# Moving the start addresses of the activation tiles in a transformer-block kernel

## The chip, the core and the metric

The kernel runs as one program on one core of a Trainium2 chip. The core has TensorE (PE; its weight loads are listed apart as PEld), VectorE (DVE), ScalarE (ACT), GpSimd (POOL) and SyncE (SP, which issues the transfers). The metric is device microseconds of one execution, lower is better. The profile comes from one further execution of the same program, taken by the hardware profiler.

## What is computed

One transformer block on 256 tokens of width 1024, all in float32: an adaptive norm whose scales, shifts and gates come from `silu(c) @ w_ada + b_ada`, a wide input projection, causal attention with eight heads of 64, a gated spatial unit, two projections and an output product with a gated residual, a second adaptive norm, a feed-forward part of width 4096 with squared ReLU, and a final norm.

```python
h = rmsnorm(x, g_mix) * (1 + scale1) + shift1
q, k, v, u, vs, ga, gb = split(h @ w_in)
y_attn = moba_attention(q, k, v) @ w_proj_attn
y_sgu  = spatial_gating(gelu(u), gelu(vs), ...) @ w_proj_sgu
x = x + gate1 * ((sigmoid(ga) * y_attn + sigmoid(gb) * y_sgu) @ w_out)
h = rmsnorm(x, g_ffn) * (1 + scale2) + shift2
x = x + gate2 * (square(relu(h @ w_ff1)) @ w_ff2)
return rmsnorm(x, g_final)
```

## The kernel before

**Products in three passes.** Each large product is made in `float32r`. A streamed weight tile `raw` of 128 x 2048 values (8,192 bytes in each partition) is rounded by ACT to `whi`, and DVE writes the rest, `raw - whi`, to `wlo`. An activation is held as such a pair too (`hh`/`hl`, `oh`/`ol`, `yh`/`yl`, `mh`/`ml`, `zh`/`zl`, `fh`/`fl`). `mm3` (L69) then issues three matmuls for one 128 x 128 block of weights: `whi` with the high part, `whi` with the low part, `wlo` with the high part. The weights are the stationary operand, and 256 columns of activations (one per token) move past them; in the feed-forward's first product it is 258 columns. So 48 matmuls belong to one streamed tile.

**The stages, in the order of the program.** First a loop over eight slices of `w_in` (L276), in which weights arrive, norm coefficients are formed, and the slice's products for q, k, v and the gate's input accumulate in eight PSUM banks; the products for v and vs have the weights as the moving operand, 512 columns each. Then ten products `n` = 0 to 9 from `hh`/`hl` (L480 on), with attention scores, exponentials, transposes and the attention's second product in between. Then four steps (n = 10 to 13) from `oh`/`ol` and `yh`/`yl`, four (n = 14 to 17) from `mh`/`ml`, and the feed-forward: 16 first products from `zh`/`zl` (`ff1`, L596) alternating with 16 second products from `fh`/`fl` (`ff2`, L628). At the end the final norm and the output.

**Order and buffers.** In the first loop and at the very end the order is the one written; in between a scheduler places the instructions, `prepare(n + 2)` (L257) making the weights of two steps later. There are five `raw` buffers, four of `whi`, three of `wlo` and eight PSUM banks (`bank`, L59). SP issues every transfer.

**Where tiles stand.** Pools are laid out one behind the other in the order in which they are opened (L51 to L56), and within a pool the tags stand in the order in which each is first asked for. A tile takes its bytes per partition, rounded up to 32. In `act` that order is `xt`/`gb_sb`/`zl` (tag b4, 8,256 bytes because of the 258 columns), `x_sb`, `hh`/`mh` (b1), `hl`/`ml` (b2), `xn`/`ga_sb`/`zh` (b3, 8,256 bytes as well), then the tiles q1, q2, v, vs, u1, o1 and o2. In `wk` it is `pt`/`fl`, `hf`, `t512b`, four `acc` of 4 bytes, `t512a`, `pr`/`fh`, and other small tiles, after which `raw`, `whi` and `wlo` begin. The profile shows no addresses; the numbers below are those of the built program.

In this text a line is 64 bytes, and the line of an address is its place among the 16 lines of 1,024 bytes. The rows of an activation tile are 1,024 bytes apart, so each row starts at the tile's own line; those of `zh` and `zl` are 1,032 bytes apart and wander by 8 bytes from one to the next. A block of 128 weights takes 512 bytes, so weights start at line 7 or line 15.

Of the kernel before, what the change touches and what calls it, by code (L numbers as in the profile page):

```python
# [9 lines left out]
F32 = mybir.dt.float32  # L10
# [6 lines left out]
P = 128  # L17
S = 256
D = 1024
KT = D // P  # L20
# [27 lines left out]
def block_kernel(ctx, tc, x, xT, cols, wsguT, bsgu, w_a1, w_1, w_a, w_m, w_f, out):  # L48
# [2 lines left out]
    const = ctx.enter_context(tc.tile_pool(name="const", bufs=1))  # L51
    act = ctx.enter_context(tc.tile_pool(name="act", bufs=1))
    wk = ctx.enter_context(tc.tile_pool(name="wk", bufs=2))
    raws = ctx.enter_context(tc.tile_pool(name="raws", bufs=5))
    his = ctx.enter_context(tc.tile_pool(name="his", bufs=4))
    los = ctx.enter_context(tc.tile_pool(name="los", bufs=3))  # L56
# [5 lines left out]
    def load(src, pieces=1):  # L62
        t = raws.tile([P, 2048], F32, name="raw", tag="raw")
        n = 2048 // pieces
        for i in range(pieces):
            nc.sync.dma_start(out=t[:, n * i:n * i + n], in_=src[:, n * i:n * i + n])
        return t
# [12 lines left out]
    for t in range(2):  # L80
        nc.sync.dma_start(out=xt[:, t, 0:D], in_=x[t])
        DVE.memset(xt[:, t, D:D + 1], (EPS * D) ** 0.5)
    x_sb = act.tile([P, KT, S], F32, name="x_sb")
    ada = {0: load(w_a1[0], 2)}
    wraw = {0: load(w_1[0], 4)}
# [33 lines left out]
                      stop=last, skip_group_check=t == 1)  # L119

    def rstd(o, n):
        ms = wk.tile([P, 2], F32, name="ms", tag="ms")
        ACT.activation(out=ms, in_=o[:, 0:2], func=AF.Identity, scale=1.0 / n, bias=eps)
        rs = wk.tile([P, 2], F32, name="rs", tag="rs")
        nc.gpsimd.tensor_tensor(out=rs, in0=ms, in1=nhalf, op=ALU.pow)
        return rs

# [50 lines left out]

    def dot(raw, i):
        junk = wk.tile([P, D], BF16, name="junk", tag="t512b")  # L180
        acc = wk.tile([P, 1], F32, name="acc", tag="acc", bufs=4)
        DVE.scalar_tensor_tensor(
            out=junk, in0=raw[:, D * i:D * i + D], scalar=0.5, in1=csb, op0=ALU.mult, op1=ALU.mult, accum_out=acc)
        return acc
# [76 lines left out]
    def ada_dots(m, half):  # L261
        i = (0, 4, 1, 5, 2, 6, 3, 7, 8, 9, 10, 11, 12, 13, 14, 15)[m]
        if half == 0:
            raw_of["d", m] = fetch("a", m)
        raw = raw_of["d", m]
        column(dot(raw, half), (SCALE2, GATE1, SHIFT2, GATE2)[i // 4], 2 * (i % 4) + half)
# [1 line left out]

    hh = act.tile([P, KT, S], F32R, name="hh", tag="b1")
    hl = act.tile([P, KT, S], F32R, name="hl", tag="b2")  # L270
    xn = act.tile([P, KT, S], F32, name="xn", tag="b3")
    wsg = const.tile([P, 8, P], F32, name="wsg", tag="c4")
    bsg = const.tile([P, NP, P], F32, name="bsg")
    qk_ps = [bank() for _ in range(4)]
# [1 line left out]
    for kt in range(KT):  # L276
# [22 lines left out]


        da = dot(raw, 0)
        if f:
            column(da, SCALE1, kt)
        db = dot(raw, 1)
        w_hi(0)
        if not f:
# [100 lines left out]

    def attn_exp(banks):
        pr = wk.tile([P, 2, 3 * P], F32, name="pr", tag="pr", bufs=3)
        sm = wk.tile([P, 2, 2], F32, name="sm", tag="sm", bufs=2)  # L410
        for i in range(2):
            b = banks[i]
            mx = wk.tile([P, 2], F32, name="mx", tag="mx", bufs=4)
            DVE.tensor_reduce(out=mx[:, 0:1], in_=b[:, 0:S], axis=AX.X, op=ALU.max, negate=True)
            DVE.tensor_reduce(out=mx[:, 1:2], in_=b[:, S:S + P], axis=AX.X, op=ALU.max, negate=True)
            ACT.activation(out=pr[:, i, 0:S], in_=b[:, 0:S], func=AF.Exp, bias=mx[:, 0:1],
                           accum_out=sm[:, i, 0:1])
            ACT.activation(out=pr[:, i, S:S + P], in_=b[:, S:S + P], func=AF.Exp, bias=mx[:, 1:2],
                           accum_out=sm[:, i, 1:2])
        return pr, sm  # L420

    def attn_norm(pr, sm):
        rc = wk.tile([P, 2, 2], F32, name="rc", tag="rc", bufs=2)
        DVE.reciprocal(out=rc, in_=sm)
        for i in range(2):
            ACT.activation(out=pr[:, i, 0:S], in_=pr[:, i, 0:S], func=AF.Copy, scale=rc[:, i, 0:1])
            ACT.activation(out=pr[:, i, S:S + P], in_=pr[:, i, S:S + P], func=AF.Copy, scale=rc[:, i, 1:2])
# [52 lines left out]
    for n in range(10):  # L480
# [23 lines left out]
        if 0 <= j < NP:  # L504
            ex[j] = attn_exp(sc.pop(j))
# [9 lines left out]
        if 0 <= j < NP:  # L515
            attn_norm(*ex[j])
# [89 lines left out]

    def relu2(o):
        r = wk.tile([P, 2, S], F32, name="r", tag="t512a")
        bw = wk.tile([P, 2], F32, name="bw", tag="bw")
        r2 = wk.tile([P, 2, S], F32, name="r2", tag="t512b")  # L610
        fh = wk.tile([P, 6 * P], F32R, name="fh", tag="pr", bufs=3)[:, 0:512].rearrange("p (i t) -> p i t", i=2)
        for i in range(2):
            DVE.tensor_copy(out=bw[:, i:i + 1], in_=o[i][:, S:S + 1])
            DVE.tensor_tensor(out=r[:, i], in0=o[i][:, 0:S], in1=rb2, op=ALU.mult)
        for i in range(2):
            ACT.activation(out=r[:, i], in_=r[:, i], func=AF.Relu, bias=bw[:, i:i + 1])
        ACT.activation(out=r2, in_=r, func=AF.Square)
        ACT.copy(out=fh, in_=r2)
        return r2, fh
# [6 lines left out]
    acc = []  # L626
# [22 lines left out]
    f[0] = ff1(slot)  # L649
    sums(ss2, sq2, True, True)  # L650
    rs2 = rstd(ss2, D)
    slot += 1
    prepare(slot + 2)
    f[1] = ff1(slot, spread2)
    a[0] = relu2(f.pop(0))
    slot += 1
    prepare(slot + 2)
    a[1] = relu2(f.pop(1))
    a[0] = relu2_low(*a[0])
    f[2] = ff1(slot)  # L660
    slot += 1
    for n in range(NU - 2):
        prepare(slot + 2)
        a[n + 1] = relu2_low(*a[n + 1])
        if n in (1, 3, 5, 7):
            ada_dots(12 + n // 2, 0)
        ff2(n, range(KT), parts[slot], a.pop(n), n == 0, False)
        a[n + 2] = relu2(f.pop(n + 2))
        slot += 1
        if n + 3 < NU:  # L670
            prepare(slot + 2)
            if n in (1, 3, 5, 7):
                ada_dots(12 + n // 2, 1)
            f[n + 3] = ff1(slot)
            slot += 1
# [41 lines left out]
    for ft in range(4, KT):  # L717
        turn(ft)
    rs3 = rstd(ss3, D)
    ys = act.tile([P, 2, D], F32, name="ys", tag="b2")  # L720
    for h in range(2):
# [54 lines left out]
```

## Time and profile before

| | |
|---|---|
| three runs | 370.91, 371.25, 371.66 us (median 371.25) |
| the profiled execution: its own time, its span | 370.36 us, 368.3 us |
| PE busy, PEld busy | 358.6 us (97%), 345.6 us (94%) |
| DVE busy, ACT busy | 259.3 us (70%), 216.4 us (59%) |
| bytes moved, mean rate | 90.39 MB, 245 GB/s |
| granted TensorE clock over the span | 0.994 |

The span runs from the first to the last instruction; the execution's own time is 2.1 us longer. Matmuls overlap one another: a row's duration (about 0.28 us) is not what a matmul costs in a stream. What it costs is the distance from its start to the start of the next. All matmuls and most other instructions are recorded under L44, the helper that pins their order, so rows are told apart by the tiles they write and read.

### The profile page before, as it was taken

Reading aid. Unit: us, or ns where it says so; the run is one execution under the profiler, and the core shown is the slowest. Engines: PE = TensorE matmul, PEld = TensorE weight load, DVE = VectorE, ACT = ScalarE, POOL = GpSimd, SP = SyncE. Lnnn points to the kernel's source line nnn. Section 1 sums busy time; section 2 is a strip of 40 time slices with the busy share of each in tenths; the row PEclk is TensorE's granted clock in tenths of the full one; section 3 lists DMA queues with packets and bytes.
Section 4 is the critical chain, followed back from the end, with each engine's and each line's share of the span. In section 5 each row is a group of like instructions: output and inputs, shape, how many; then the busy total and the mean of one; then the engine's idle time right before and its main releaser. Section 6 shows DMA issues by size and latency. Waiting matters only on the chain.

```text
span 368.3 us, 6942 instructions
## 1 busy us (share of the span) xinstructions
PE 358.6 (97%) x2898; PEld 345.6 (94%) x2898; DVE 259.3 (70%) x397; ACT 216.4 (59%) x308; POOL 9.5 (3%) x16
## 2 busy tenths in 40 slices
PE   6999999999999999999999999999999999999993
PEld 4888879999999999999999999999999999999993
DVE  4888888589799968999758575576665644645443
ACT  4856569899954563555576554465544664445242
POOL 3000000003000000000000000000000000000001
PEclk9999999999999999999999999999999999999997
DMA  7999999699999886478654675746647464500003
GB/s 252 418 414 414 403 331 379 251 346 364 335 345 385 314 315 238 188 255 328 217 159 185 219 253 215 274 183 237 253 198 299 159 230 154 190 2 0 2 0 114
DMA packets 16270, 90.39 MB, mean 245 GB/s; under 512 B 1904, under 2 KB 2416, under 8 KB 7152
## 3 DMA queue, kind: packets, MB, share of 16 engines
q1 hardware_dynamic: 16240, 89.97, 65.7%
q8 instruction: 22, 0.36, 0.4%
q14 instruction: 8, 0.07, 0.0%
HBM read 88.91 MB, written 1.05 MB: 244 GB/s over the span
## 4 chain that ended last, share of the span: by engine, by line
PE 83%; DMA 9%; DVE 4%; issue 1%; ACT 1%; POOLq 0%; POOL 0%; DVEq 0%; SPq 0%
PE bank L44 83%; DMA raw<-in_w 5%; DVE junk L44 3%; DMA raw<-in_w_a 2%; DMA raw<-in_w_m 1%; DMA cols_sb<-in_cols 0%; DVE wlo L44 0%; ACT hf L44 0%; ACT whi L44 0%; DVE x_sb L44 0%; POOLq L772 0%; DVE ys L44 0%; POOL sq L699 0%; DVE sq L44 0%; DVEq L772 0%
## 5 line engine op out<-in xcount | busy, mean ns | idle before, releaser
L44 ACT CAST whi<-raw 128x2048 fp32r<-128x2048 f32 (+2 forms) x74 | 112.8, 1538 | 79.8 <-PE bank L44 75.3
L44 DVE TENSOR_TENSOR wlo<-raw,whi 128x2048 fp32r<-128x2048 f32 (+2 forms) x74 | 134.4, 1826 | 15.2 <-ACT whi L44 14.8
L44 PE MATMUL bank<-zh,whi 128*128 128x258 f32 x256 | 72.6, 283 | 0.0
L44 PE MATMUL bank<-zl,whi 128*128 128x258 f32 x256 | 72.4, 283 | 0.0
L44 PE MATMUL bank<-fh,wlo 128*128 128x256 f32 x256 | 72.2, 282 | 0.0
L44 PE MATMUL bank<-zh,wlo 128*128 128x258 f32 x256 | 72.1, 282 | 0.0
L44 PE MATMUL bank<-fh,whi 128*128 128x256 f32 x256 | 71.9, 281 | 0.0
L44 PE MATMUL bank<-fl,whi 128*128 128x256 f32 x256 | 71.5, 279 | 0.0
L44 DVE SCALAR_TENSOR_TENSOR junk<-raw,csb 128x1024 bf16<-128x1024 f32 x48 | 57.3, 1217 | 0.0
L44 PE MATMUL bank<-hh,whi 128*128 128x256 f32 x224 | 55.9, 289 | 0.3
L44 PE MATMUL bank<-hl,whi 128*128 128x256 f32 x224 | 54.4, 282 | 0.2 <-DVE hl L44 0.2
L44 PE MATMUL bank<-hh,wlo 128*128 128x256 f32 x224 | 54.4, 282 | 0.0
L44 PEld LDWEIGHTS bank<-zh,wlo 128*128 128x128 f32 x256 | 48.4, 189 | 0.0
L44 PEld LDWEIGHTS bank<-zl,whi 128*128 128x128 f32 x256 | 48.4, 189 | 0.0
L44 PEld LDWEIGHTS bank<-fl,whi 128*128 128x128 f32 x256 | 48.3, 189 | 0.0
L44 PEld LDWEIGHTS bank<-zh,whi 128*128 128x128 f32 x256 | 48.3, 189 | 0.0
L44 PEld LDWEIGHTS bank<-fh,whi 128*128 128x128 f32 x256 | 48.1, 188 | 0.0
L44 PEld LDWEIGHTS bank<-fh,wlo 128*128 128x128 f32 x256 | 48.0, 188 | 0.0
L44 PEld LDWEIGHTS bank<-hh,whi 128*128 128x128 f32 x224 | 38.5, 188 | 4.4 <-ACT hh L44 3.4
L44 PEld LDWEIGHTS bank<-hl,whi 128*128 128x128 f32 x224 | 38.4, 188 | 0.5 <-DVE hl L44 0.4
L44 PEld LDWEIGHTS bank<-hh,wlo 128*128 128x128 f32 x224 | 38.4, 188 | 0.0
L44 DVE TENSOR_TENSOR fl<-r,fh 128x512 fp32r<-128x512 f32 x16 | 11.1, 693 | 30.2 <-PE bank L44 28.9
(143 smaller groups left out, 478.6 us busy)
## 6 DMA issues: line engine op xcount, KB each, us to landing
raw<-in_w_f SPq DMA_DIRECT2D x32, 1024.0 KB, 4.9
raw<-in_w_a SPq DMA_DIRECT2D x22, 1024.0 KB, 7.4
raw<-in_w_m SPq DMA_DIRECT2D x16, 1024.0 KB, 7.2
raw<-in_w SPq DMA_DIRECT2D x12, 512.0 KB, 9.5
raw<-in_w_a SPq DMA_DIRECT2D x4, 512.0 KB, 6.5
raw<-in_w SPq DMA_DIRECT2D x8, 256.0 KB, 6.6
xt<-in_x SPq DMA_DIRECT2D x2, 512.0 KB, 3.9
raw<-in_w_m SPq DMA_DIRECT2D x4, 256.0 KB, 5.5
```

Source lines behind the costliest of these rows:

```text
L44: return lambda *a, **k: pin(op(*a, **k))
```

## The change

The new pool `small` is opened behind `wk` and takes the tiles of 4 to 16 bytes (`ms`, `rs`, `acc`, `sm`, `mx`, `rc`, `bw`) out of `wk`. The tile `xn` (tag b3) is asked for ahead of `x_sb` instead of behind `hh` and `hl`. No instruction, order, wait or transfer is added, removed or moved on any engine; only addresses differ.

```diff
+    small = ctx.enter_context(tc.tile_pool(name="small", bufs=2))
...
+    xn = act.tile([P, KT, S], F32, name="xn", tag="b3")
     x_sb = act.tile([P, KT, S], F32, name="x_sb")
...
-        ms = wk.tile([P, 2], F32, name="ms", tag="ms")
+        ms = small.tile([P, 2], F32, name="ms", tag="ms")
...
-        acc = wk.tile([P, 1], F32, name="acc", tag="acc", bufs=4)
+        acc = small.tile([P, 1], F32, name="acc", tag="acc", bufs=4)
...
-    xn = act.tile([P, KT, S], F32, name="xn", tag="b3")
```

The tiles `rs`, `sm`, `mx`, `rc` and `bw` are edited in the same way. In `act` the second tile of 8,256 bytes now stands ahead of `x_sb`, `b1` and `b2`, which moves these by one line; in `wk` the four `acc` no longer stand ahead of `t512a` and `pr`, which moves these back by two lines. The start lines in the built programs:

| tile | line before | line after |
|---|---|---|
| `hh`, `hl`, `mh`, `ml` | 13 | 14 |
| `oh`, `ol`, `yh`, `yl` | 14 | 14 |
| `fh` (three buffers) | 0 | 14 |
| `fl` (two buffers) | 14 | 14 |
| `zh` | 13, wandering | 13, wandering |
| `zl` | 12, wandering | 12, wandering |
| `whi`, `wlo`, `raw` | 7 | 7 |

## Rows read from the trace of the kernel before

**Rows 1.** The chain that ended last: start, length (us), what.
```profile
39.35 7.06 DMA raw<-in_w_a
...
55.08 301.39 PE bank L44 x2544
356.48 0.03 issue
356.50 0.89 DVE x_sb L44 x2
```
**Rows 2.** Waits of PE, then of PEld: total us, times, longest.
```profile
PE bank L44 <- DVE hl L44: 0.2, 1, 0.2
PEld bank L44 <- ACT mh L44: 0.2, 1, 0.2
```
**Rows 3.** PE in order of time: start, length (us), tiles; nine places.
```profile
60.34 0.28 PE L44 MATMUL bank<-hh,whi 128*128 128x256 f32 x1
...
65.92 0.28 PE L44 MATMUL bank<-hh,wlo 128*128 128x256 f32 x1
...
130.84 0.28 PE L44 MATMUL bank<-oh,whi 128*128 128x256 f32 x1
...
152.61 0.28 PE L44 MATMUL bank<-mh,whi 128*128 128x256 f32 x1
...
164.24 0.28 PE L44 MATMUL bank<-mh,whi 128*128 128x256 f32 x1
...
169.94 0.28 PE L44 MATMUL bank<-mh,whi 128*128 128x256 f32 x1
...
250.85 0.28 PE L44 MATMUL bank<-fh,whi 128*128 128x256 f32 x1
...
256.51 0.28 PE L44 MATMUL bank<-zh,whi 128*128 128x258 f32 x1
...
262.27 0.28 PE L44 MATMUL bank<-fh,whi 128*128 128x256 f32 x1
```
**Rows 4.** Stretches: length, busy us of each engine (x instructions), clock, DMA share, GB/s.
```profile
80.00:100.00 20.00, 20.00 (x176) 18.54 (x177) 16.84 (x34) 19.14 (x50) 3.13 (x1) 1.00 0.94 342
...
140.00:160.00 20.00, 20.00 (x174) 19.83 (x173) 18.02 (x22) 8.79 (x10) 0.00 (x0) 1.00 0.58 211
...
240.00:260.00 20.00, 20.00 (x171) 20.00 (x170) 13.99 (x18) 11.51 (x12) 0.00 (x0) 1.00 0.58 213
```
**Rows 5.** PE around the start of the product n = 4.
```profile
88.49 0.82 PE L44 MATMUL bank<-ident,pr 128*128 128x128 f32 x6
89.24 0.87 PE L44 MATMUL bank<-pt,v_sb 128*64 128x256 f32 x8
90.04 0.39 PE L44 MATMUL bank<-hh,whi 128*128 128x256 f32 x1
```
**Rows 6.** ACT: where its unbroken work begins, and at n = 4.
```profile
67.64 0.72 ACT L44 ACTIVATE vs_sb<-vs_sb,vrs 128x512 f32<-128x512 f32 x1 [1.01 <-POOL vrs L512]
...
85.50 1.49 ACT L44 ACTIVATE pr<-pr,rc 128x256 f32<-128x256 f32 x4
...
89.14 0.36 ACT L44 ACTIVATE pr<-bank,mx 128x128 f32<-128x128 f32 x1
```
**Rows 7.** DVE, then ACT, then PE behind the product n = 13.
```profile
152.81 0.69 DVE L44 SCALAR_TENSOR_TENSOR yg<-gb_sb,bank 128x512 f32<-128x512 f32 x1 [0.57 <-PE bank L44]
153.42 2.28 DVE L44 TENSOR_TENSOR wlo<-raw,whi 128x2048 fp32r<-128x2048 f32 x1
156.34 0.62 ACT L44 CAST mh<-yg 128x512 fp32r<-128x512 f32 x1 [1.58 <-DVE yg L44]
157.01 0.39 PE L44 MATMUL bank<-mh,whi 128*128 128x256 f32 x1
```
**Rows 8.** PE in the last slice: the products for v and vs begin.
```profile
57.57 0.39 PE L44 MATMUL bank<-whi,hh 128*128 128x512 f32 x1
```
**Rows 9.** Three neighbours in a first feed-forward product.
```profile
250.12 0.29 PE L44 MATMUL bank<-zh,whi 128*128 128x258 f32 x1
250.25 0.29 PE L44 MATMUL bank<-zl,whi 128*128 128x258 f32 x1
250.38 0.28 PE L44 MATMUL bank<-zh,wlo 128*128 128x258 f32 x1
```
**Rows 10.** The closest weight tile: DVE makes it, PE uses it.
```profile
70.19 2.29 DVE L44 TENSOR_TENSOR wlo<-raw,whi 128x2048 fp32r<-128x2048 f32 x1 [2.26 <-ACT whi L44]
74.33 0.28 PE L44 MATMUL bank<-hh,wlo 128*128 128x256 f32 x1
```

More of the change, by code (lines that the diff above doesn't have):

```diff
@@ L121, in rstd @@
     def rstd(o, n):
-        ms = wk.tile([P, 2], F32, name="ms", tag="ms")
+        ms = small.tile([P, 2], F32, name="ms", tag="ms")
         ACT.activation(out=ms, in_=o[:, 0:2], func=AF.Identity, scale=1.0 / n, bias=eps)
-        rs = wk.tile([P, 2], F32, name="rs", tag="rs")
+        rs = small.tile([P, 2], F32, name="rs", tag="rs")
         nc.gpsimd.tensor_tensor(out=rs, in0=ms, in1=nhalf, op=ALU.pow)
@@ L409, in attn_exp @@
         pr = wk.tile([P, 2, 3 * P], F32, name="pr", tag="pr", bufs=3)
-        sm = wk.tile([P, 2, 2], F32, name="sm", tag="sm", bufs=2)
+        sm = small.tile([P, 2, 2], F32, name="sm", tag="sm", bufs=2)
         for i in range(2):
             b = banks[i]
-            mx = wk.tile([P, 2], F32, name="mx", tag="mx", bufs=4)
+            mx = small.tile([P, 2], F32, name="mx", tag="mx", bufs=4)
             DVE.tensor_reduce(out=mx[:, 0:1], in_=b[:, 0:S], axis=AX.X, op=ALU.max, negate=True)
@@ L422, in attn_norm @@
     def attn_norm(pr, sm):
-        rc = wk.tile([P, 2, 2], F32, name="rc", tag="rc", bufs=2)
+        rc = small.tile([P, 2, 2], F32, name="rc", tag="rc", bufs=2)
         DVE.reciprocal(out=rc, in_=sm)
@@ L608, in relu2 @@
         r = wk.tile([P, 2, S], F32, name="r", tag="t512a")
-        bw = wk.tile([P, 2], F32, name="bw", tag="bw")
+        bw = small.tile([P, 2], F32, name="bw", tag="bw")
         r2 = wk.tile([P, 2, S], F32, name="r2", tag="t512b")
```

## The prediction

> **What bounds the kernel now.** I read the chain of waits first, since it says whose time is the kernel's. Up to 55 us it passes through transfers; from 55.08 us it is one piece of 301.39 us on PE, ending at 356.47 us, where the final norm begins [rows 1]. So for 82% of the span anything that makes a matmul cheaper shortens the program, if nothing else becomes late. Next the waits of PE and its weight loads: behind 55 us none is longer than 0.2 us, and the two shown stand at the last slice and at the products from `mh` [rows 2]. In the stretches the granted clock is 1.00, the 2.4 GHz level [rows 4].
>
> At 2.4 GHz, 256 columns take 256 / 2.4 = 106.7 ns. What a matmul costs is the distance between starts, read in nine places [rows 3]:
>
> - from `hh`/`hl`, n = 0: 48 matmuls, first start 60.34, last 65.92, so 5.58 us / 47 = 118.7 ns;
> - from `oh`/`ol` and `yh`/`yl`, four steps: 130.84 to 152.61, 21.77 us / 192 = 113.4 ns;
> - from `mh`/`ml`, n = 16: 164.24 to 169.94, 5.70 / 48 = 118.75 ns;
> - one `ff2`: 250.85 to 256.51, 5.66 / 48 = 117.9 ns;
> - one `ff1` (258 columns): 256.51 to 262.27, 5.76 / 48 = 120.0 ns.
>
> The first four are the same instruction: 128 x 128 weights, 256 columns of `float32r`, three passes, weights at lines 7 and 15. They differ in the activations' start line: 13, 14, 13, and 0 for `fh` with 14 for `fl`. The steps from line 14 are the cheapest, and they lie between dearer ones. Load on the other engines does not sort them: in the stretch 140 to 160, mostly line 14, DVE is busy 18.02 of 20 us, and in 240 to 260, where `ff1` and `ff2` alternate, 13.99, with equal DMA shares of 0.58 [rows 4]. So I take the start line as the cause, and 113.4 ns as the cost at line 14.
>
> The Trainium skill's page "TensorE: Matmul & The Clock Gate" (Part 2, "Step-by-step: what each phase is for") speaks against such an effect: PE has two independent read ports into SBUF, and loading the next weights takes no read bandwidth from the running matmul. Its section "Wait — 56ns, not 53.3ns?" gives columns / 2.4 plus about 2.5 ns, so as an estimate from that page 109.2 ns for 256 columns wherever they start. The starts above, 113.4 against 118.7 ns for one shape, do not agree with that. By the rule alone the change is worth nothing, which is the rival "no change" below.
>
> **The change part by part.** No engine gets another instruction, wait or place in its order, and no queue another transfer, so only durations can change.
>
> *`hh` and `hl`, line 13 to 14.* Ten steps, n = 0 to 9, with 47 distances each (the 48th leads into other work): 470 x (118.72 - 113.39 ns) = 2.51 us. In the last slice only what stands behind 55.08 us counts, 20 matmuls of 256 columns: 20 x 5.33 = 0.11 us. Earlier slices wait for weights, so there it is worth nothing.
>
> The twelve matmuls with weights moving run from 57.57 to 60.34 us, 231 ns each for 512 columns [rows 3, 8]. There the stationary operand is what moves by a line, a pairing that no row shows. Bounds: twice 113.4 is 226.8 ns, a gain of 0.05 us over twelve; the dearest neighbours I found, 0.26 us for two distances, 130 ns each [rows 9], give 260 ns and a loss of 0.35 us. Nearest are twice 117.9 or so, within 0.06 us of now; I take zero and keep both ends.
>
> *`mh` and `ml`, line 13 to 14.* 192 x (118.75 - 113.39) = 1.03 us.
>
> *`fh`, line 0 to 14, beside `fl` already there.* Sixteen `ff2`, 768 x (117.92 - 113.39) = 3.48 us.
>
> *`zh`, `zl`.* They keep lines 13 and 12, so 768 matmuls stay at 120.0 ns. *The small tiles, `x_sb`, `xn`, `t512a`:* other engines' operands. No row compares ACT or DVE at two lines; I cost this at nothing, since from 55 to 356 us both run beside PE, and keep 0.3 us to either side for the tail, where they stand on the path.
>
> Sum on PE: 2.51 + 0.11 + 1.03 + 3.48 = 7.13 us.
>
> **What becomes late.** PE runs ahead, and whatever it waits for does not run faster.
>
> *The bank of n = 4.* ACT works without a pause from 67.64 us, where it waited for POOL, to beyond 89.5 us [rows 6], so a faster PE does not pull it forward. The built program gives the product n = 4 the PSUM bank from which ACT reads a score tile until 89.14 + 0.36 = 89.50 us; PE starts that product at 90.04 [rows 5, 6]. The cover is 0.54 us. By then PE has gained 0.11 + 4 x 47 x 5.33 ns = 1.11 us, so it waits some 0.57 us. The transposes ahead of it have more: `pr` is done at 85.50 + 1.49 = 86.99, PE takes it from 88.49.
>
> *`mh` for n = 14.* The products of n = 13 end at 152.61 us. Behind them DVE does `yg`, a `wlo` of 2.28 us and another sum, then ACT casts `mh`, done at 156.34 + 0.62 = 156.96; PE takes it at 157.01 after 36 matmuls [rows 3, 7]. That latency hangs on PE's end and stays, and 36 matmuls become 36 x 5.36 = 0.19 us shorter, so 0.19 us of the gain turns into waiting.
>
> *Weights.* The closest tile is `wlo` of n = 2, done at 70.19 + 2.29 = 72.48 us and used at 74.33 [rows 10]: 1.85 us against a gain of about 0.6 by then. Later ones are made further ahead. DMA is at 0.94 in 80 to 100 us [rows 4]; a PE two per cent faster asks for little more, and the weights in hand cover it.
>
> Net: 7.13 - 0.57 - 0.19 = 6.37 us. The profiled execution took 370.36 us, so 363.99; it lies 0.89 us below the median of 371.25. From the median, which new runs are to be held against, 371.25 - 6.37 = 364.9 us, and that is the forecast.
>
> **The rivals.**
>
> *ACT takes over in the attention stage.* ACT is busy 19.14 of 20 us in 80 to 100 [rows 4]. If the whole stage is paced by it and not only at n = 4, the 2.62 us from `hh` are lost: 1.03 - 0.19 + 3.48 = 4.32 us are left, 366.9 us. Against it: apart from the bank of n = 4 I see covers of 1.5 us or more there. For it: I checked covers against the old times, and waits can chain.
>
> *The feed-forward keeps its cost.* If 117.9 ns comes from the way `ff2` walks its weights (blocks of one output 4,096 bytes apart, in four banks) and not from line 0, 3.48 us are lost: 371.25 - 2.89 = 368.4 us. Against it: `fl` is at line 14 already and its pass is no cheaper by itself, which fits a mixed pair as well.
>
> *No change.* Start lines do not matter, and the cheap stage is cheap for something else in n = 10 to 13: 371.25 us. Against it: `mh` and `oh` steps differ in nothing else that I can see.
>
> *More than forecast.* By its name the change puts all activations on line 14. If `ff1` came along, 768 x (120.0 - 113.4) = 5.07 us more, 359.8 us. Against it stand the sizes: 8,256 bytes before `zh`, and rows of 1,032.
>
> *Slower.* In `ff2` the high and the low part now both start one line short of a weight block in every buffer. If loads and columns then meet in the same place each time, the distance rises instead of falling. The rest gains 2.89 us, so the kernel is slower once `ff2` passes 117.9 + 2.89 / 768 = 121.7 ns; at the 130 ns of [rows 9] it would be 768 x 12.1 = 9.3 us lost, 371.25 + 9.3 - 2.9 = 377.7 us. Against it: `oh` and `yh` stand on these very lines, and cost least.
>
> **How the numbers follow.** Forecast 0.77; ACT takes over 0.09; feed-forward unchanged 0.05; no change 0.04; slower 0.03; more 0.02. A measurement of this kernel can tell about 0.2%, 0.74 us, from no change. All but two of the cases are faster by more: 0.93; the same 0.04; slower 0.03. The forecast's own range is 363.6 to 366.0 us: no new waits at all would give 364.1, the v products at their dear end 365.2, the tail 0.3 us, and a median moves by some 0.4 us. For 8 in 10 I reach out to the ACT case: 363.4 to 367.4 us.
>
> **What would show it.** Right: starts in steps from `hh`, `mh` and `fh` at 113 to 114 ns, in `ff1` still at 120; PE idle for about half a microsecond ahead of n = 4, released by ACT; the wait for `mh` at n = 14 grown by 0.2 us; the tail as long as before. The forecast is wrong if `ff2` stays above 116 ns, if `hh` steps at 113 ns are followed by gaps at several n, or if `ff1` moves.

## The result, and the profile after

The changed kernel takes 365.12 us (median of five runs, 364.80 to 365.55), the kernel before 371.25 (five runs, 370.90 to 371.66): a ratio of 0.9846, interval 0.9834 to 0.9858. The forecast was 364.9 us. The profiled executions stand 5.04 us apart, 370.36 and 365.32: the one of before lies 0.89 us under its median, the one of after 0.20 over.

The chain of waits after (start us, length us, what) answers to [rows 1]:

```profile
55.61 96.11 PE bank L44 x832
...
155.27 0.63 ACT mh L44
155.95 195.52 PE bank L44 x1676
351.49 0.89 DVE x_sb L44 x2
```

PE still owns it. It is cut once now, where PE waits for `mh` of n = 14, and it begins 0.53 us later than before. That start comes out of the weight transfers of the first stage and not out of the change: on the chain the last of them ends at 51.24 us, and in another execution of the same changed program at 50.70, with PE's start at 55.05.

Where the time went is read by stage, each from its first PE start to the next stage's: `hh` n = 0 to 9, then `oh`/`yh`, then `mh`, then the feed-forward. First before, then after (stretch, length, busy us of PE, PEld, DVE, ACT, POOL, granted clock, DMA share, GB/s):

```profile
60.34:130.84 70.50, 70.50 (x610) 67.04 (x608) 60.11 (x109) 52.62 (x99) 3.83 (x2) 1.00 0.90 337
130.84:152.61 21.77, 21.77 (x194) 21.77 (x193) 17.23 (x17) 12.01 (x10) 0.00 (x0) 1.00 0.65 241
152.61:175.63 23.02, 23.02 (x195) 22.85 (x193) 22.09 (x37) 12.46 (x16) 0.00 (x0) 1.00 0.76 273
175.63:359.13 183.50, 183.50 (x1547) 183.50 (x1546) 108.94 (x148) 96.34 (x107) 1.10 (x2) 1.00 0.47 171
```
```profile
60.75:129.79 69.04, 69.04 (x610) 65.53 (x608) 59.17 (x109) 52.76 (x99) 3.61 (x2) 1.00 0.91 339
129.79:151.55 21.76, 21.76 (x195) 21.76 (x193) 18.24 (x18) 12.01 (x10) 0.00 (x0) 1.00 0.71 264
151.55:173.74 22.19, 22.03 (x195) 21.84 (x194) 21.99 (x37) 12.47 (x16) 0.00 (x0) 1.00 0.77 274
173.74:354.01 180.27, 180.27 (x1546) 180.27 (x1545) 109.06 (x149) 96.42 (x107) 0.98 (x2) 1.00 0.48 175
```

The clock is what it was, and the DMA share nearly so. The stages change by -1.46, -0.01, -0.83 and -3.23 us. With -0.12 in the last slice (5.26 to 5.14 us) and nothing in the tail (9.13 us both times, in spans of 368.26 and 363.14) that is -5.65 us from the chain's start on PE to the end.

PE's starts after (start, length, tiles) answer to [rows 3]:

```profile
67.31 0.36 PE L44 MATMUL bank<-hh,whi 128*128 128x256 f32 x1
67.51 0.28 PE L44 MATMUL bank<-hl,whi 128*128 128x256 f32 x1
...
72.93 0.28 PE L44 MATMUL bank<-hh,wlo 128*128 128x256 f32 x1
...
124.35 0.28 PE L44 MATMUL bank<-hh,whi 128*128 128x256 f32 x1
...
129.68 0.28 PE L44 MATMUL bank<-hh,wlo 128*128 128x256 f32 x1
...
162.51 0.28 PE L44 MATMUL bank<-mh,whi 128*128 128x256 f32 x1
...
167.96 0.28 PE L44 MATMUL bank<-mh,whi 128*128 128x256 f32 x1
...
247.97 0.28 PE L44 MATMUL bank<-fh,whi 128*128 128x256 f32 x1
...
253.42 0.29 PE L44 MATMUL bank<-zh,whi 128*128 128x258 f32 x1
...
259.18 0.28 PE L44 MATMUL bank<-fh,whi 128*128 128x256 f32 x1
```

`mh`: 5.45 us / 48 = 113.5 ns. `ff2`: 5.45 / 48 = 113.5. `ff1`: 5.76 / 48 = 120.0, as before. `hh` has both: n = 9 takes 5.33 / 47 = 113.4 ns, but n = 1, behind its first distance, 5.42 / 46 = 117.8. Over all ten steps n = 1 to 4 and n = 7 lie at 117.7 to 117.8, the others at 113.3 to 113.9. Nothing is in between: behind its first six matmuls each of these steps is at one level and stays there.

### The profile page after: what moved, and what is told of

Read it like the earlier page. It is cut to its first block, busy times and chain, and to the rows that moved or that the text cites. A ratio compares the mean times of both kernels' runs of the same rounds, so it can differ in the third digit from the quotient of the medians.

```text
span 363.1 us, 6942 instructions
## 1 busy us (share of the span) xinstructions
PE 352.5 (97%) x2898; PEld 339.3 (93%) x2898; DVE 259.5 (71%) x397; ACT 216.5 (60%) x308; POOL 9.1 (3%) x16
## 4 chain that ended last, share of the span: by engine, by line
PE 80%; DVE 6%; ACT 5%; DMA 3%; issue 3%; SPq 1%; DVEq 0%; POOLq 0%; POOL 0%
PE bank L44 80%; DVE junk L44 3%; DMA raw<-in_w 2%; ACT whi L44 2%; DVE wlo L44 2%; DMA raw<-in_w_m 1%; ACT hh L44 1%; ACT hf L44 1%; ACT bcol L44 1%; SPq L67 0%; DVE yg L44 0%; DVE x_sb L44 0%; SPq L82 0%; DVE ys L44 0%; POOLq L773 0%
## 5 line engine op out<-in xcount | busy, mean ns | idle before, releaser
L44 PE MATMUL bank<-fh,whi 128*128 128x256 f32 x256 | 70.7, 276 | 0.0
L44 PE MATMUL bank<-fh,wlo 128*128 128x256 f32 x256 | 70.7, 276 | 0.0
L44 PE MATMUL bank<-fl,whi 128*128 128x256 f32 x256 | 70.7, 276 | 0.0
L44 PE MATMUL bank<-hh,wlo 128*128 128x256 f32 x224 | 53.6, 279 | 0.0
```

What stands on the lines that cost most here:

```text
L44: return lambda *a, **k: pin(op(*a, **k))
```

## The experiments

The theory: the distance between starts depends on the lines at which activations and weights begin relative to one another, inside TensorE. The rivals: absolute lines, the other engines' load, or something else that the change moves.

**Each half of the change alone, and the weights moved after it.** The first keeps only the new pool, the second only the earlier `xn`, the third has the whole change and moves all weight tiles by a further line.

```diff
# first                            # second
+small = tile_pool("small", 2)     +xn = act.tile(... tag="b3")   # ahead of x_sb
-ms = wk.tile(...)   (and 6 more)  -xn = act.tile(... tag="b3")   # behind hl
+ms = small.tile(...)
# third: the change, and ahead of raws
+pad = tile_pool("pad", 1)
+DVE.memset(pad.tile([P, 16], F32), 0.0)
```

> Only the pool for the small tiles: fh goes from line 0 to 14, hh and mh stay at 13. Line theory (the cost hangs on the start line of the activations against that of the weights): ff2 steps at 113.5 ns a matmul, hh and mh steps at 118.7 as before; 768 x 4.4 ns = 3.3 us less than before, 367.9 us. Rival (ff2 is cheap only together with something the other half of the change brings): ff2 stays near 118 ns and the time at 371.

> Only xn ahead of x_sb: hh and mh go to line 14, fh stays at 0. Line theory: mh at 113.3 ns, hh on average 115.6 ns with single steps at either 113.4 or 117.7, ff2 at 117.9; 1.1 + 0.8 us less than before, 369.3 us. Rival (the slower hh steps come from what the faster neighbours make of the load on ACT and DVE): hh steps all alike.

> The changed kernel with 64 bytes put in ahead of raw, whi and wlo: weights at line 8 instead of 7, activations still at 14. Relative theory (activation line minus weight line, here 6 as hh had before): hh, mh, oh, yh and fh all near 118.7 ns, so about 192 x 5.3 ns = 1.0 us for oh and yh, 1.0 for mh, 4.0 for ff2 and 1.6 for hh over the changed kernel, 372 to 373 us with zh unknown. Absolute theory (line 14 is cheap by itself): 113.4 ns stays and the time is 365.1.

Before takes 371.03 us on that chip. The first takes 367.36 (ratio 0.9897, 0.9880 to 0.9914): `ff2` at 113.55 ns, `hh` and `mh` about as before, at 119.2 (before 118.9) and 118.7. The second takes 368.89 (0.9940, 0.9924 to 0.9956): `hh` at 115.3 on average, `mh` at 113.4, `ff2` unchanged at 117.87. Their gains, 3.67 and 2.14 us, add up to 5.81, against 6.13 for both together. One `ff2` block in PE's order, of the first and of the second:

```profile
195.20 0.28 PE L44 MATMUL bank<-fh,whi 128*128 128x256 f32 x1
...
200.65 0.29 PE L44 MATMUL bank<-zh,whi 128*128 128x258 f32 x1
```
```profile
191.93 0.28 PE L44 MATMUL bank<-fh,whi 128*128 128x256 f32 x1
...
197.58 0.28 PE L44 MATMUL bank<-zh,whi 128*128 128x258 f32 x1
```

5.45 us against 5.65 for 48 matmuls. The third takes 372.78 us (1.0048, 1.0034 to 1.0062). The activations stand on line 14 as after the change, yet the whole gain is gone and the cheap stage of before is lost too. The four steps from `oh` and `yh`:

```profile
131.19:153.97 22.78, 22.78 (x195) 22.78 (x193) 17.24 (x17) 11.99 (x10) 0.00 (x0) 1.00 0.65 234
```

22.78 / 192 = 118.6 ns, with other engines as busy as before. "Line 14 is the cheap one" is thereby refuted; what counts is where it stands to the weights.

**All of it one line further.** The pad stands ahead of the `act` pool, so activations go to 15 and weights to 8.

```diff
+DVE.memset(pad.tile([P, 16], F32), 0.0)   # pool ahead of act
```

> The changed kernel with 64 bytes put in ahead of all activations, so that every activation and every weight stands one line further on: hh, mh, oh, yh, fh, fl at 15, weights at 8. Relative theory: distances as in the changed kernel (mh, oh, ff2 at 113.4 ns), 365.1 us within 0.7. If line 14 or line 7 counted by itself, mh, oh and ff2 would leave 113.4 ns and the time would go towards 371.

365.34 us (0.9852, 0.9825 to 0.9880): `oh` and `mh` at 113.33 ns, `ff2` at 113.55, `ff1` at 120.03. The relation decides, not the absolute line. In `hh` the dear level came at n = 1, 3 and 7 only.

**TensorE alone.** The weights stand at lines 7 and 15, the activations at each of eight lines; the kernel's three passes run 48 matmuls each, behind none or a few other matmuls ("entries").

```diff
+for e in ENTRIES:
+    for a, c, b, st, n in CASES:     # lines of high, low, weights
+        entry(e)
+        ...  # 16 x: (wh, ah), (wh, al), (wl, ah), n columns
```

> TensorE alone, no block computed: 48 matmuls in three passes as in the kernel, for each start line 0 to 7 of the activations with weights at 7 and 15, with 256 and 258 columns, each behind four different entries. If the lines set the cost inside TensorE: 113.4 ns at line 6 (or 117.7 behind some entries), 118 to 119 at lines 5 and 0, something between 107 and 123 at the others. If the cost comes from other engines' traffic in the shared memory: one level near 107 to 109 ns for all lines, since nothing else runs.

In a span of 497.7 us DVE is busy for 0.3 us, and ACT for 14.1, none of it between 16.3 and 487 us. Mean distance in the last 24 of 48, with 256 columns (without line 0 behind the first entry, where the granted clock was at 0.5 for a time):

| line | 0 | 1 | 2 | 3 | 4 | 5 | 6 | 7 |
|---|---|---|---|---|---|---|---|---|
| ns | 117.8 (113.3) | 118.6 | 113.3 (117.8) | 120.0 | 117.8 | 118.7 | 113.3 | 120.0 |

In brackets stands what one of the entries gave instead. Lines 6, 7, and then line 0 behind two entries (25th and 48th start of each):

```profile
55.09 0.28 PE L24 MATMUL o<-ah,wh 128*128 128x256 f32 x1
...
57.70 0.28 PE L24 MATMUL o<-ah,wl 128*128 128x256 f32 x1
...
60.68 0.28 PE L24 MATMUL o<-ah,wh 128*128 128x256 f32 x1
...
63.44 0.28 PE L24 MATMUL o<-ah,wl 128*128 128x256 f32 x1
...
135.17 0.28 PE L24 MATMUL o<-ah,wh 128*128 128x256 f32 x1
...
137.88 0.28 PE L24 MATMUL o<-ah,wl 128*128 128x256 f32 x1
...
251.76 0.28 PE L24 MATMUL o<-ah,wh 128*128 128x256 f32 x1
...
254.37 0.28 PE L24 MATMUL o<-ah,wl 128*128 128x256 f32 x1
```

Over 23 distances: 2.61 us = 113.5 ns, 2.76 = 120.0, and for the same line 0 once 2.71 = 117.8 and once 2.61 = 113.5. So the effect needs no other engine; but for the choice of level it repeats every four lines as far as tried (14 is 6 and 2, 13 is 5 and 1); and lines 0 and 2 have two levels, of which one or the other comes by the matmuls ahead. High rows on line 0 with low rows on line 6, the pair that `ff2` had before, gave 117.1 to 117.8 ns. At 258 columns nothing fell to 113: 118.6 to 122.3 ns.

**Four lines apart from one another.** The same loop with `whi` and `wlo` at lines of their own, 64 pairings, 36 matmuls, three entries.

```diff
+CASES = [(a, c, 7, d, ...) for a in range(4) for c in range(4) for d in range(4, 8)]
```

> TensorE alone, no block computed: 36 matmuls for each of 64 pairings of the high rows' line, the low rows' line and wlo's line (whi at 7), each behind three entries. Two-level theory: pairings with high and low rows and both weights in step show either 113.3 or 117.8 ns, odd distances 118.7 or 120; a pairing that is at 113.3 behind all three entries would be the place for hh. If each pass had a cost of its own, mixed pairings would show the mean of their passes.

One pairing of 64 is at 113.3 to 113.4 ns behind all three entries: activations at 2, `whi` at 7, `wlo` at 5. The kernel's own (2, 2, 7, 7) gives 117.8, 117.8 and 113.3. The last 18 starts of the two behind the first entry:

```profile
193.79 0.28 PE L24 MATMUL o<-ah,wh 128*128 128x256 f32 x1
...
195.72 0.28 PE L24 MATMUL o<-ah,wl 128*128 128x256 f32 x1
...
202.18 0.28 PE L24 MATMUL o<-ah,wh 128*128 128x256 f32 x1
...
204.18 0.28 PE L24 MATMUL o<-ah,wl 128*128 128x256 f32 x1
```

1.93 / 17 = 113.5 against 2.00 / 17 = 117.6. Besides these two only activations at 0, with `wlo` at 7 or 5, reach 113.3 or 113.4, behind one entry each; all others lie between 115.6 and 121.3 ns (here and below without the very first stream, where the granted clock was at 0.5 for a time). A pass has no cost of its own: high rows at 2, low rows at 0 and `wlo` at 5 give 120.6 to 120.8 ns, though (2, 2, 7, 5) is at 113.3 and (0, 0, 7, 7) at 117.8 or less.

In the loop before this one even and odd lines wrote to different PSUM banks. Here lines 0 to 3 with both weights at 7 write to the same pair of banks, and the pattern stays: 117.8 or 113.3, 118.8, 117.8 or 113.3, 120.0 ns. Nor does the entry alone set the level: the same two short matmuls gave line 2 the upper one there and the lower one here.

**`wlo` two lines off, in the kernel.** The change, and 128 bytes ahead of `los`.

```diff
+DVE.memset(pad.tile([P, 32], F32), 0.0)   # between his and los
```

> The changed kernel with 128 bytes put in ahead of wlo alone: activations at 14, whi at 7, wlo at 9, the one pairing that was at 113.3 ns behind every entry. Two-level theory (the dear hh steps are the other of two levels that a stream can fall into, chosen by its entry): all ten hh steps at 113.4 to 113.8 ns, five steps x 47 x 4.4 ns = 1.0 us less than the changed kernel, less some 0.5 us of waiting for a PSUM bank at n = 4; oh, mh and ff2 stay at 113.4; 364.1 to 364.6 us if zh stays at 120. Rival (the dear steps come from the load of ACT and DVE in those steps): n = 1 to 4 and 7 stay at 117.7 ns, 365.1 us.

364.92 us (0.9843, 0.9820 to 0.9866). All ten `hh` steps are at 113.3 to 114.7 ns, and the wait at n = 4 is there (idle ahead and its releaser in brackets):

```profile
89.67 0.36 ACT L44 ACTIVATE pr<-bank,mx 128x128 f32<-128x128 f32 x1
...
90.17 0.19 PEld L44 LDWEIGHTS bank<-hh,whi 128*128 128x128 f32 x1 [0.77 <-ACT pr L44]
90.18 0.38 PE L44 MATMUL bank<-hh,whi 128*128 128x256 f32 x1 [0.53 <-ACT pr L44]
```

ACT ends the score tile's exp at 90.03, and PE starts 0.15 us later, after 0.53 us of idling. So nearly all that the single level gives ahead of n = 4 is lost there, and the time can't be told from the changed kernel's.

**The 258 columns of `ff1`.** First with one or two of the three passes cut to 256, then 64 pairings of lines.

```diff
+# first: columns of the passes (258, 258, 258), (258, 256, 258), (256, 256, 256 or 258)
+# then:  CASES = [(h, l, 7, d, ... 258, 258, 258) for h in range(4) for l in range(4) for d in range(4, 8)]
```

> TensorE alone, no block computed: the first feed-forward product's passes with 258 columns in all three, or 256 in the low pass, or 258 in the first alone, over start lines. With 258 columns in all three 119 to 122 ns as in the kernel; if what is dear is the 17th line that 258 columns touch, each pass cut to 256 columns saves up to 6.7 ns of its own, 2.2 ns a matmul for one pass and 4.4 for two.

> TensorE alone, no block computed: 258 columns in all passes with rows 1,032 bytes apart, for 64 pairings of the lines of high rows, low rows and wlo. From the earlier table 119 to 121 ns; if the two-level picture holds for wandering rows too, none is under 118, and the pairing of the kernel (lines 1, 0 of four, wlo at 7) is near 120.

The idea that two columns more open a 17th line and cost the 6.5 ns by that is not borne out: with the low pass cut, the mean over the entries is still 118.7 to 120.5 ns, with two passes cut 117.8 to 120.1. It is fully tested for the low pass alone, since the high rows stayed 1,032 bytes apart and touch a 17th line at 256 columns too. Of the 64 pairings none is under 118 ns: 118.8 to 121.0, the kernel's own 120.2. What holds 258 columns above 113 stays open.

**The best lines found, beside the changed kernel.** `wlo` as above, and pads that put `zh` on 15, `zl` on 13, `wlo` on 1, `whi` on 15 and the other activations on 6. The second run is the changed kernel itself.

```diff
+DVE.memset(act.tile([P, 16], F32), 0.0)   # ahead of xt, another ahead of xn
+DVE.memset(act.tile([P, 96], F32), 0.0)   # ahead of x_sb
```

> Lines chosen from the tables: as the kernel with wlo two lines on, and zh at three lines, zl at one line modulo four (zh 15, zl 13, whi 15, wlo 1; all other activations 6). TensorE alone showed 119.0 ns for that pairing with 258 columns, against 119.8 in the kernel with wlo two lines on: 768 x 0.8 ns = 0.6 us less than that kernel, 364.3 us; hh, oh, mh and ff2 at 113.4 to 114. If the tables taken with nothing else running do not carry over, ff1 stays at 119.8 to 120 ns.

> The changed kernel again, for comparison on one chip: 365.1 us; mh, oh and ff2 at 113.4 ns, ff1 at 120.0. Two-level theory: the hh steps at either 113.4 to 113.9 or 117.7 ns, not necessarily the same steps as in the first profile.

364.17 us (363.65 to 365.09; ratio 0.9820, 0.9795 to 0.9845) against 365.37 (364.75 to 366.08; 0.9851, 0.9829 to 0.9872), five runs each on one chip: 1.2 us less, though the two ranges overlap by a run and the intervals of the ratios overlap too, so the times alone do not settle it. `ff1` falls from 120.0 to 119.06 ns; one block of it:

```profile
196.65 0.28 PE L44 MATMUL bank<-zh,whi 128*128 128x258 f32 x1
...
202.36 0.28 PE L44 MATMUL bank<-fh,whi 128*128 128x256 f32 x1
```

5.71 / 48 = 119.0 ns; times 768 that makes 0.72 us, the larger part of the 1.2. The repeated changed kernel showed something else: its `hh` steps are dear at n = 1, 2, 3 and 7, with n = 4 cheap this time, and `mh` steps that were cheap in the first profile are dear:

```profile
162.37 0.28 PE L44 MATMUL bank<-mh,whi 128*128 128x256 f32 x1
...
168.02 0.28 PE L44 MATMUL bank<-mh,whi 128*128 128x256 f32 x1
```

5.65 / 48 = 117.7. There the level changed within a step: the first 36 matmuls of n = 14 stand 113.3 ns apart, and all of them behind the wait for `mh` 117.8. The whole stage takes 22.88 us, against 23.02 before and 22.19 in the first profile:

```profile
150.80:173.68 22.88, 22.72 (x195) 22.53 (x193) 22.09 (x37) 12.46 (x16) 0.00 (x0) 1.00 0.76 271
```

The same program falls into either level in different executions.

## Why the prediction was right, and which step failed

- **The cause**: right. Each half moved its own products and nothing else, and one line of the weights took all of it back. The reason given in the prediction, line 14 as such, was too narrow: it is the distance to the weights, which "line 14" stood for because they never moved.
- **`ff2`, 3.48 us**: 3.31 (768 distances, 90.52 to 87.21 us). **`mh`, 1.03 less 0.19**: 0.83, with the weight load's wait for `mh` grown from 0.2 to 0.4 us; but only 0.14 in the repeated run, so the hit was luck of the execution. **Last slice, 0.11**: 0.12. **v products, tail and `ff1` at zero**: the twelve v products take 2.75 us against 2.77, the tail is as long as before, `ff1` 120.0 ns as before.
- **`hh`, "470 x (118.72 - 113.39 ns) = 2.51 us": this step failed.** Five of ten steps went to 117.75 ns, not to 113.39, which keeps 5 x 47 x 4.36 ns = 1.02 us; the stage gave 1.46. The step took four `oh`/`yh` stretches, all at the lower level, as the cost of the line; the line has two. A sign of it stood in the trace of before, from which the prediction read n = 0 alone: on line 13 too n = 8 and 9 are at 120.0 ns and the other eight at 118.5 to 118.7. First and last start of n = 9 before the change, 5.64 / 47 = 120.0 ns:

```profile
125.08 0.28 PE L44 MATMUL bank<-hh,whi 128*128 128x256 f32 x1
...
130.72 0.28 PE L44 MATMUL bank<-hh,wlo 128*128 128x256 f32 x1
```

- **The bank of n = 4, 0.57 us**: nearly nothing after the change, because the gain that was to reach it was not there. These rows, in order of time, show how near it was; below them stands the last attention matmul of the kernel before:

```profile
89.65 0.36 ACT L44 ACTIVATE pr<-bank,mx 128x128 f32<-128x128 f32 x1
89.89 0.27 PE L44 MATMUL bank<-pt,v_sb 128*64 128x128 f32 x1
...
90.16 0.19 PEld L44 LDWEIGHTS bank<-hh,whi 128*128 128x128 f32 x1 [0.24 <-ACT pr L44]
90.16 0.39 PE L44 MATMUL bank<-hh,whi 128*128 128x256 f32 x1
```
```profile
89.84 0.27 PE L44 MATMUL bank<-pt,v_sb 128*64 128x128 f32 x1
```

ACT ends at 90.01, and 0.15 us behind it PE starts, as in the run where PE idled. PE's start lies 0.27 us behind the last attention matmul, where it was 0.20 before (89.84 to 90.04), so ACT held it up by some 0.07 us, which shows as no idling because matmuls overlap. The cover was thus 0.54 - 0.15 = 0.39 us and was used up. With the lower level in all steps PE idled for 0.53 us. The wait was rightly found, but that its size came out near 0.57 is partly luck: 0.15 us of the cover was not there, and the gain by then was some 0.39 + 0.53 = 0.92 us, not 1.11. Stage by stage the two errors partly cancel: 1.94 us forecast net, 1.46 found.
- **The rivals.** ACT holds PE up at n = 4 at most, not over the stage; the feed-forward did not keep its cost; `ff2` did not rise; `ff1` did not come along.

From one execution to another the sum is 5.65 us on the path, or 5.12 of the span with the later start of the chain (5.04 of the execution's own time). The medians fell by 6.13. That the prediction's 6.37 lies so close to this is partly luck, since the levels and the start vary between executions by some tenths of a microsecond, which one profile of each can't resolve.

The Trainium skill, "TensorE: Matmul & The Clock Gate" (Part 2, "Step-by-step: what each phase is for"), says that loading the next weights doesn't steal read bandwidth from the running matmul. With TensorE running alone, 113.3 to 120.0 ns for one shape by start lines alone doesn't fit a load that never meets the columns. The measurement decides: where the two begin relative to one another matters. That it is the reads of weights and columns that meet is argued from this, and no run showed it directly.

## What to carry to other kernels

Where PE is the path and its starts lie further apart than the columns take, sort the distances by where both operands begin; stages of one shape with two costs in one trace are the sign. Move one operand by 64 bytes, in steps over four lines, and measure in the kernel, since pads cost only memory. Before counting a gain, look for a second level within a stage, and count the cover of each buffer that PE will then reach earlier.

## What the runs showed that was not expected

- One shape (128 x 128 weights, 256 columns, three passes) takes 113.3, 117.8, 118.6 or 120.0 ns by start lines modulo four, with nothing else running, as long as both parts of the activations stand on one line and both weights on one; mixed pairings have values in between and up to 121.3.
- At the good lines there are two levels, 113.3 and 117.8 ns, held, behind the first few, for streams of 36 to 192 matmuls. Which one depends on the matmuls ahead, and for the same program on the execution. With activations on line 2 of four, the high and low weights two lines apart gave the lower level behind every entry tried and in all ten steps. The kernel before had two levels as well, 118.6 and 120.0 ns on line 13. Why an entry picks a level stays open.
- 258 columns cost 118.6 to 122.3 ns at every pairing tried, 5 ns or more above the best of 256.
